# A two-layer decoder trunk on one core: where x is kept, how one of Strassen's sums is made, what is loaded first, two parts of w_so and the last norm

## The chip, the core and the metric

The kernel is one program on one of the eight cores of a Trainium2 chip. The core has a matrix engine (PE, TensorE), a vector engine (DVE), a scalar engine (ACT), a general engine (POOL, GpSimd) and a sequencer that mostly issues loads and stores (SP). Each engine runs its own instructions in a fixed order and waits on semaphores of the others; DMA queues move data between the device memory and the core's memory (SBUF). PE adds up its results in eight banks (PSUM) that DVE and ACT read. The metric is the device time of one execution in microseconds; the time before is 1018.95 us, the median of three runs.

## The reference

512 tokens of 1024 features go through two layers, all in float32. A layer is a mixer and an MLP, each with a scaled residual and a norm:

```python
for l in range(2):
    if l == 0:
        y = mla(x, w_in, g_q, g_kv, w_uq, w_uk, w_uv, w_o)      # 8 heads, latent keys and values, causal
    else:
        k_band, v_band = shared_kv(x, w_kv)                     # once
        y = swa(x, w_q, sinks, w_so, k_band, v_band, rel_bias)  # 16 heads, window 128, sinks
    x = layernorm(sqrt(2) * x + y, ln_mix_g[l], ln_mix_b[l])
    h = relu(x @ w_up[l])                                       # 1024 -> 4096
    x = layernorm(sqrt(2) * x + (h * h) @ w_down[l], ln_mlp_g[l], ln_mlp_b[l])
```

## The kernel before

**Split products.** A float32 operand is written as a high and a low part (`split`, L76: ACT rounds the high part, L78, DVE or POOL subtracts it, L81). A product is then three matmuls, high by high, high by low, low by high (`three`, L101; `group`, L95, issues them, so nearly all matmuls have line L97). In the profile `xth`, `xtl` are the parts of the features, `wh`, `wl` those of a weight, `fac` both parts of the MLP's hidden features, `oh`, `ol` those of a head pair's output.

**The stream of weights.** All weights are queued in one list, `stream`, in the order in which PE uses them. A tile (128x1024) is loaded into `raw` by SP and split into a ring of four `wh`, `wl` pairs; `weights` (L276) hands out the next pair and prepares up to four ahead. A split into the ring must wait until PE has read the old content of its place for the last time. The MLP uses Strassen's seven products for quarters of the up and down matrices (`queue_seven`, L147): their sums of quarters grow in place in `wq` by DMAs that POOL issues and that add to what is there (L170), each followed by a split of the grown tile.

**Layer A's mixer.** The features of x arrive transposed (xT) and are loaded and split piece by piece together with w_kv, then w_q, each on SP's queue and in the order of the program. The compressed keys and queries are normed (L802 on), transposed and kept as `ckv_h`, `ckv_l`, `cq_h`, `cq_l`; `pair_rotary` (L946) turns the rotary part of a pair of heads from `qrot` through one of the two banks for transposes (`tr`). `run_steps` (L475) sets the order by hand: scores some units ahead, softmax, mix, and between them `fill` entries, which are other PE work. The output matrix w_o is in parts, `proj.part(t, kp)`, for token tile t and two of eight heads kp.

**Norms.** `layer_norm` (L362) takes mean and variance on DVE, adds epsilon on DVE (L369), takes the inverse root on POOL (L350), and scales on DVE (L380, L383). The last tile of the last norm is divided: 832 columns on DVE, 192 on ACT and POOL (L376 to L379), and out by SP and ACT. In layer A, x's token tiles are loaded after its mixer.

**The MLP.** Block q of four runs steps of up products (U'n) and down products (D'n) in the order of `STEPS`; the first block's are U'1 U'2 U'5 U'3 U'6 U'7 U'4 D'1 D'2. `XFactors` makes the seven sums of x's quarters: `XFactors.turn` (L584) transposes a token tile, and at the last tile L560 and L562 form part 3's sum, then parts 3, 6, 7, 4 are split one after the other. The results of U'6, U'7, U'4 become the quarters a11, a21, a22 of the hidden features, squared on ACT (L692 relu, L693 square), then split into `fac` (`factor`) for D'1. `up_out` (L666) takes the sums out of PSUM on DVE.

Banks, rings and tiles are given out by a scheduler that puts each engine's instructions into one order before the run.

Of the kernel before, what the change touches and what calls it, by code (L numbers as in the profile page):

```python
# [8 lines left out]
F32 = mybir.dt.float32  # L9
# [6 lines left out]
P = 128  # L16
# [20 lines left out]
LN_CUT_END = 832  # L37

# [12 lines left out]
def build(tc, nc, io, out):  # L51
    with ExitStack() as top:
# [3 lines left out]
        sp = top.enter_context(tc.tile_pool(name="sp", bufs=1))  # L56
        ps = top.enter_context(tc.tile_pool(name="ps", bufs=1, space=PSUM))
# [18 lines left out]
        def split(dst_h, dst_l, src, engine=None, keep=False):  # L76

            high = nc.scalar.activation(dst_h, src, AF.Copy)  # L78
            if keep:
                pe(high)  # L80
            low = (engine or nc.vector).tensor_sub(dst_l, src, f32(dst_h))  # L81
            if pinned[0] and engine is None:
                pe(low)

# [3 lines left out]
        pinned = [False]  # L88

# [16 lines left out]

        def tiles_of_weights(aside=None):
# [10 lines left out]
        def queue(name, ap, low=nc.vector):  # L118


            def make(pieces=1, between=None):
                cols = ap.shape[-1]
                raw = raw_tile()
                wh, wl = tiles_of_weights()
                for j in range(pieces):
# [3 lines left out]
                    pe(nc.sync.dma_start(raw[:, c], ap[:, c]))  # L129
                    split(wh[:, c], wl[:, c], raw[:, c], low)  # L130
                return wh, wl

            stream.append((name, make))
# [13 lines left out]
        def queue_seven(name, key, chunk):  # L147
# [5 lines left out]
            def half(a, jp):  # L153
                if a not in quads:
                    if (key, a) == ("U", "a"):
                        quads[a] = xp.tile([P, 4, 512], F32, tag="xt", bufs=8, name=nm("wq"))
                    elif (key, a) == ("U", "b"):
                        quads[a] = xtok.tile([P, 4, 512], F32, tag="gb", bufs=1, name=nm("wq"))
# [7 lines left out]
            def grown(a, jp, *more, aside=None):  # L166
                wh, wl = tiles_of_weights(aside)
                split(wh, wl, flat(half(a, jp)), keep=(a, bool(more)) == ("b", True) and key == "U")
# [46 lines left out]
        queue("w_qr", io["w_qr"][0])  # L215
        queue("w_qr", io["w_qr"][1][:, 0:512])
# [102 lines left out]
        def load_x(k, n):  # L319
            at = k // 4, slice(k % 4, k % 4 + n)  # L320
            src = xraw[at[0]][:, at[1], :]
            nc.sync.dma_start(src, io["xT"][:, k : k + n, :])
# [10 lines left out]
        nc.sync.dma_start(ident, io["ident"])  # L333
        gq = cp.tile([P, 3], F32, name="gq")
        nc.sync.dma_start(gq, io["g_q"])
        gkv = cp.tile([P, 2], F32, name="gkv")
        nc.sync.dma_start(gkv, io["g_kv"])
        sink = cp.tile([P, SQH], F32, name="sink")
        nc.sync.dma_start(sink, io["sinks"].partition_broadcast(P))
        relb = cp.tile([33, SQH], F32, name="relb")  # L340
        nc.gpsimd.memset(relb[32:33, :], 1.0)
        nc.sync.dma_start(relb[0:32, :], io["rel"])
# [13 lines left out]
        def load_gb(g, b):  # L356
            gb = xtok.tile([P, 2, D], F32, tag="gb", bufs=1, name=nm("gb"))
# [4 lines left out]
        def layer_norm(t, gb, dst):  # L362
# [8 lines left out]
            end = dst is None and t == NT - 1  # L371
            cut = LN_CUT_END if end else D
            a, b = slice(0, cut), slice(cut, D)
            if end:
                shift = sp.tile([P, 1], F32, tag="v", bufs=8, name=nm("v"))
                nc.vector.tensor_scalar(shift, mv[:, 0:1], r, -1.0, ALU.mult, ALU.mult)  # L376
                nc.scalar.activation(x[:, b], x[:, b], AF.Identity, bias=shift, scale=r)
                nc.gpsimd.tensor_mul(x[:, b], x[:, b], gb[:, 0, b])
                nc.gpsimd.tensor_add(x[:, b], x[:, b], gb[:, 1, b])  # L379
            pin(nc.vector.scalar_tensor_tensor(x[:, a], x[:, a], mv[:, 0:1], gb[:, 0, a], ALU.subtract, ALU.mult))  # L380
            pieces = [slice(0, cut // 2), slice(cut // 2, cut)] if end else [a]
            for c in pieces:
# [3 lines left out]
            if end:  # L386
                nc.scalar.dma_start(out[t * P : (t + 1) * P, b], x[:, b])
# [22 lines left out]
        class TokMajor:  # L410
# [25 lines left out]
            def finish(self, gb=None, dst=None, early=None):  # L436
# [7 lines left out]
                if gb is not None:  # L444
                    ws = [weights(self.name) for _ in range(4)]
                    for t in range(NT):
# [28 lines left out]
        def run_steps(units, ahead, scores, turn, mix, fill, per, lag):  # L475
# [17 lines left out]
            for f in fill[at:]:  # L493
                f[3]()
            for u in range(n, n + lag):
# [5 lines left out]
        def count(t, c):  # L501
# [4 lines left out]
            for i in range(c.start // n, c.stop // n):  # L506
                pin(nc.vector.bn_stats(stats[t][:, i, :], xs[t][:, i * n : (i + 1) * n]))  # L507

# [60 lines left out]
        class XFactors(Factors):  # L569
# [14 lines left out]
            def turn(self, t):  # L584
                half_, tk = t // 2, slice(t % 2 * P, (t % 2 + 1) * P)
                if t % 2 == 0:
# [11 lines left out]
                if half_ == 1:  # L598
# [3 lines left out]
                    split(self.part(5, 0)[:, :, tk], self.part(5, 1)[:, :, tk], self.a[:, :, tk], keep=True)  # L602
                if t == NT - 1:
                    state["hold"] = len(stream)
                    quarters = [f32(self.xf[i][:, n]) for i in range(2) for n in range(2)]
                    for n in (3, 6, 7, 4):
                        split(self.part(n, 0), self.part(n, 1), self.sum(n, *quarters))

        def mlp(src, gb, dst, mp):
# [17 lines left out]
            class Block:  # L627
# [38 lines left out]
                def up_out(self, n, i):  # L666
# [114 lines left out]
        with tc.tile_pool(name="mla", bufs=1) as mp:  # L781
            const = mp.tile([P, C_ALL], F32, name="const")
            nc.sync.dma_start(const, io["const"])
# [4 lines left out]
            ckv_l = mp.tile([P, 2, S], F32R, name="ckv_l")  # L788
            khh = mp.tile([P, S], F32R, name="khh")
            kll = mp.tile([P, S], F32R, name="kll")  # L790
            cq_h = mp.tile([P, 3, S], F32R, name="cq_h")
# [570 lines left out]
```

## Time and profile before

| | |
|---|---|
| median of the runs | 1018.95 us (1017.45 to 1023.35) |
| the profiled execution | 1022.03 us, span 1020.2 us |
| mean granted clock of PE | 0.995 |
| PE busy, idle in the span | 995.0 us, 25.2 us |
| DVE, ACT, POOL busy | 766.3, 555.2, 229.9 us |
| software queue, accumulating loads of up | 64 of 512 KB, median 8.6 us to landing |

A row of the timeline has start, length, engine, line, operation, output<-input, shapes and count, and in brackets the idle time of the engine before it with what ended it. A row of the windows gives, for a stretch of time, the busy microseconds (and count) of each engine, then PE's granted clock, the DMA engines' share and their GB/s.

### The profile page before, as it was taken

How to read it: one execution, taken by the hardware profiler on the slowest of the kernel's cores; microseconds unless marked ns; L12 is line 12 of the kernel's file. 1: busy time of each engine (PE TensorE's matmuls, PEld its weight loads, DVE VectorE, ACT ScalarE, POOL GpSimd, SP SyncE). 2: the span in 40 equal slices, each digit the busy share in tenths (PEclk: the TensorE clock that was granted, in tenths of full speed). 3: DMA queues.
4: the chain of work that ended last, by engine and by line, in shares of the span. 5: the costliest groups of instructions: out<-in, count | busy, mean ns of one | idle time of the engine just before them, and what ended most of it. 6: DMA issues, size and time to landing. Idle time of an engine off the chain costs nothing. (4 is left out here: it accounts for less than half of the span.)

```text
span 1020.2 us, 15872 instructions
## 1 busy us (share of the span) xinstructions
PE 995.0 (98%) x6148; PEld 894.7 (88%) x6148; DVE 766.3 (75%) x1230; ACT 555.2 (54%) x848; POOL 229.9 (23%) x204
## 2 busy tenths in 40 slices
PE   8999999999999999999999999999999999999996
PEld 7878887898989989998889888889999999998985
DVE  4688875979869858887595578588886885798746
ACT  4446653457637636646145689445764664564620
POOL 0121100321211211220013665223032132122002
PEclk9999999999999999999999999999999999999999
DMA  6531116397986986973332223237798798798422
GB/s 211 159 99 45 52 42 231 59 247 195 198 182 186 194 182 171 252 138 109 99 103 94 66 81 114 81 86 201 169 219 179 164 222 167 167 264 150 108 99 82
DMA packets 60391, 149.55 MB, mean 147 GB/s; under 512 B 5228, under 2 KB 10141, under 8 KB 60317
## 3 DMA queue, kind: packets, MB, share of 16 engines
q0 software_dynamic: 24320, 58.73, 32.3%
q1 hardware_dynamic: 35852, 89.72, 26.3%
q8 instruction: 48, 0.79, 0.3%
q14 instruction: 27, 0.21, 0.1%
q10 hardware_dynamic: 144, 0.10, 0.0%
HBM read 146.41 MB, written 4.22 MB: 148 GB/s over the span
## 5 line engine op out<-in xcount | busy, mean ns | idle before, releaser
L97 PE MATMUL mm<-wh,fac 128*128 128x512 f32 (+1 forms) x944 | 293.0, 387 | 0.4 <-DVE fac L81 0.4
L78 ACT ACTIVATE wh<-wq 128x1024 fp32r<-128x1024 f32 x164 | 173.1, 1059 | 191.9 <-PE mm L97 123.9
L81 DVE TENSOR_TENSOR wl<-wq,wh 128x1024 fp32r<-128x1024 f32 x164 | 199.4, 1221 | 76.7 <-ACT wh L78 75.8
L97 PE MATMUL mm<-xth,wh 128*128 128x256 f32 (+1 forms) x936 | 245.8, 290 | 0.6 <-DVE a L687 0.5
L97 PE MATMUL mm<-xth,wl 128*128 128x256 f32 (+1 forms) x808 | 235.4, 291 | 0.0
L97 PEld LDWEIGHTS mm<-wh,fac 128*128 128x128 f32 x944 | 176.1, 188 | 36.6 <-DVE fac L81 1.9
L97 PE MATMUL mm<-xtl,wh 128*128 128x256 f32 (+1 forms) x680 | 199.7, 294 | 3.5 <-DVE xtl L81 3.5
L97 PE MATMUL mm<-wl,fac 128*128 128x512 f32 (+1 forms) x472 | 182.3, 386 | 0.0
L97 PEld LDWEIGHTS mm<-xth,wh 128*128 128x128 f32 x936 | 170.8, 192 | 4.0 <-issue 0.9
L97 PEld LDWEIGHTS mm<-xth,wl 128*128 128x128 f32 x808 | 155.4, 192 | 2.3
L78 ACT ACTIVATE wh<-raw 128x1024 fp32r<-128x1024 f32 (+4 forms) x89 | 87.9, 989 | 105.1 <-PE mm L97 59.2
L170 POOL DMA_DIRECT2D wq<-in_up x64 | 77.5, 1225 | 266.4 <-DVE wl L81 197.8
L97 PEld LDWEIGHTS mm<-xtl,wh 128*128 128x128 f32 x680 | 130.9, 192 | 7.1 <-DVE xtl L81 4.1
L81 DVE TENSOR_TENSOR wl<-raw,wh 128x1024 fp32r<-128x1024 f32 (+4 forms) x70 | 80.2, 1154 | 52.1 <-ACT wh L78 52.0
L97 PEld LDWEIGHTS mm<-wl,fac 128*128 128x128 f32 x472 | 88.8, 188 | 16.7
L170 POOL DMA_DIRECT2D wq<-in_down x48 | 42.0, 874 | 190.5 <-DVE wl L81 170.3
L350 POOL TENSOR_TENSOR rs<-v,half 128x1 f32<-128x1 f32 x24 | 28.6, 1190 | 201.5 <-DVE v L369 160.7
L81 POOL TENSOR_TENSOR wl<-raw,wh 128x1024 fp32r<-128x1024 f32 (+1 forms) x19 | 40.1, 2117 | 85.2 <-ACT wh L78 85.2
L97 PE MATMUL mm<-wl,oh 128*128 128x512 f32 x128 | 50.1, 391 | 0.7 <-DVE wl L81 0.7
L97 PE MATMUL mm<-wh,oh 128*128 128x512 f32 x128 | 50.7, 396 | 0.0
L97 PE MATMUL mm<-wh,ol 128*128 128x512 f32 x128 | 50.1, 391 | 0.0
L513 DVE TENSOR_TENSOR x<-mm,x 128x512 f32<-128x512 f32 (+1 forms) x49 | 32.9, 675 | 13.9 <-PE mm L97 13.6
(220 smaller groups left out, 1838.9 us busy)
## 6 DMA issues: line engine op xcount, KB each, us to landing
wq<-in_up POOLq DMA_DIRECT2D x64, 512.0 KB, 8.6
wq<-in_down POOLq DMA_DIRECT2D x48, 512.0 KB, 7.0
wq<-in_up SPq DMA_DIRECT2D x32, 512.0 KB, 5.8
raw<-in_down SPq DMA_DIRECT2D x28, 512.0 KB, 7.3
wq<-in_down SPq DMA_DIRECT2D x24, 512.0 KB, 7.1
raw<-in_up SPq DMA_DIRECT2D x16, 512.0 KB, 4.9
raw<-in_w_o SPq DMA_DIRECT2D x8, 512.0 KB, 3.3
raw<-in_w_sq SPq DMA_DIRECT2D x8, 512.0 KB, 3.4
```

Of the source, the lines that this page charges most:

```text
L78: high = nc.scalar.activation(dst_h, src, AF.Copy)
L81: low = (engine or nc.vector).tensor_sub(dst_l, src, f32(dst_h))
L97: pe(nc.tensor.matmul(dst, st, mv, start=first and i == 0, stop=last and i == len(pairs) - 1, **kw))
L170: nc.gpsimd.dma_start(half(a, jp), chunk(*more, jp), accum_op=ALU.add)
L350: nc.gpsimd.tensor_tensor(r, v, half, ALU.pow)
L513: nc.vector.tensor_add(xs[t][:, c], b, xs[t][:, c])
```

## The change

x's token tiles get their own pool, whose four places hold layer A's queries (`cq`, `qrot`) until the last of them is read; so x is loaded before layer A's end, and the mixer's gamma and beta after four more weight tiles. At the start the loads of w_kv's last two and w_q's four tiles go ahead of the small constants, through two tiles of the ring `xt` that are unused so far (`fetch`), and `pe` fixes SP's order. w_qr's low parts are subtracted by POOL. `pair_rotary` uses a bank of the matmuls. Epsilon is added to one of the batch statistics, so that the inverse root follows the variance directly. The last norm runs on DVE, in one pass and then two halves. Part 3's sum is built from a difference made at the start of the last turn, in two halves; parts 6, 7 and 4 move into `rest`, called by the first block's U'5 and ordered behind the last weight split issued by then. Two parts of w_o run before the last mix, and two parts of w_so some heads earlier.

```diff
-        queue("w_qr", io["w_qr"][0])
-        queue("w_qr", io["w_qr"][1][:, 0:512])
+        queue("w_qr", io["w_qr"][0], nc.gpsimd)
+        queue("w_qr", io["w_qr"][1][:, 0:512], nc.gpsimd)
...
+        spare = [xp.tile([P, 2, 1024], F32, tag="xt", bufs=8, name=nm("spare")) for _ in range(2)]
         for kp in range(1, 4):
             load_x(2 * kp, 2)
+            if kp > 1:
+                fetchers[kp](spare[0][:, kp - 2, :])
             prep(kp)
+        for i in range(4, 8):
+            fetchers[i](spare[1][:, i - 4, :] if i < 6 else raw_tile())
...
-            v = sp.tile([P, 1], F32, tag="v", bufs=8, name=nm("v"))
-            pin(nc.vector.tensor_scalar(v, mv[:, 1:2], LN_EPS, None, ALU.add))
-            r = rsqrt_of(v)
...
+            r = rsqrt_of(mv[:, 1:2])
+            pin(nc.vector.scalar_tensor_tensor(x, x, mv[:, 0:1], gb[:, 0, :], ALU.subtract, ALU.mult))
+            n = 2 if dst is None and t == NT - 1 else 1
+            for i in range(n):
+                c = slice(i * D // n, (i + 1) * D // n)
                 pin(nc.vector.scalar_tensor_tensor(x[:, c], x[:, c], r, gb[:, 1, c], ALU.mult, ALU.add))
...
+                if t == NT - 1:
+                    self.b = self.scratch()
+                    with tc.issue_after(self.low[1].ins):
+                        nc.vector.tensor_sub(self.b, f32(self.xf[0][:, 1]), f32(self.xf[0][:, 0]))
...
                 if t == NT - 1:
+                    for i in (1, 0):
+                        tk = slice(i * P, (i + 1) * P)
+                        if i == 0:
+                            with tc.issue_after(self.low[1].ins):
+                                nc.vector.tensor_add(self.b[:, :, tk], self.b[:, :, tk], self.a[:, :, tk])
+                        state["s4"] = split(self.part(3, 0)[:, :, tk], self.part(3, 1)[:, :, tk], self.b[:, :, tk], keep=True)
                     state["hold"] = len(stream)
-                    quarters = [f32(self.xf[i][:, n]) for i in range(2) for n in range(2)]
-                    for n in (3, 6, 7, 4):
-                        split(self.part(n, 0), self.part(n, 1), self.sum(n, *quarters))
+
+            def rest(self):
+
+                a11, _, a21, a22 = [f32(self.xf[i][:, n]) for i in range(2) for n in range(2)]
+                with behind(state["last"]):
+                    nc.vector.tensor_sub(self.a, self.a, a11)
+                    split(self.part(6, 0), self.part(6, 1), self.a)
+                    nc.vector.tensor_sub(self.b, a11, a21)
+                    split(self.part(7, 0), self.part(7, 1), self.b)
+                    split(self.part(4, 0), self.part(4, 1), a22)
...
                     w = [weights("up") for _ in range(2)]
+                    if (self.q, n) == (0, 5):
+                        src.rest()
...
                         if i == 1:
-                            nc.scalar.activation(self.g["a12"], self.g["a12"], AF.Square)
+                            with behind(state.pop("s4") if self.q == 0 else None):
+                                nc.scalar.activation(self.g["a12"], self.g["a12"], AF.Square)
...
+            cq = [xtok.tile([P, 2, S], F32R, tag="x", bufs=NT, name=nm("cq")) for _ in range(2)]
+            cq.append(mp.tile([P, 2, S], F32R, name="cq2"))
+            qrot = [xtok.tile([P, 2, 512], F32, tag="x", bufs=NT, name=nm("qrot")) for _ in range(2)]
+
+            def load_x_tokens():
+                for t in range(NT):
+                    xs[t] = xtok.tile([P, D], F32, tag="x", bufs=NT, name=nm("x"))
+                    pe(nc.sync.dma_start(xs[t], io["x"][t * P : (t + 1) * P, :]))
...
-                pt = tbank()
+                pt = bank()
...
+            fill.append((0, 99, -9, load_x_tokens))
...
+            run_steps([(h, i) for h in range(H) for i in range(NT)], AHEAD_S, scores, turn, mix, fill, NT, 2,
+                      [lambda kp=kp: proj.part(2, kp) for kp in range(2)])
...
-                    fill.append((1.3, 99, (11, 14)[t] + kp, lambda t=t, kp=kp: proj.part(t, kp)))
+                    at = 11 if (t, kp) < (0, 2) else (11, 14)[t] + kp
+                    fill.append((1.3, 11 if at == 11 else 99, at, lambda t=t, kp=kp: proj.part(t, kp)))
```

Three places show what this does to the order on an engine. The first is ACT in layer A's MLP, around the sums of x's quarters. `uv_456_2232` is part 3's sum before, `uv_449_2158` part 6's, `xf_446_2145` part 7's source; the `wq` tiles are the grown sums of w_up. Before:

```order
L78 ACTIVATE wh_461_2274<-wq_460_2272 128x1024
L78 ACTIVATE wh_463_2280<-wq_460_2272 128x1024
L78 ACTIVATE xth_457_2236<-uv_449_2158 128x1024
L78 ACTIVATE xth_450_2160<-uv_456_2232 128x1024
L78 ACTIVATE wh_465_2285<-wq_407_1908 128x1024
L78 ACTIVATE xth_459_2243<-xf_446_2145 128x1024
L78 ACTIVATE wh_469_2340<-wq_407_1908 128x1024
L78 ACTIVATE wh_471_2345<-wq_460_2272 128x1024
```

and of the change, where part 3's sum is `uv_452_2215` and part 6's `uv_447_2157`:

```order
L77 ACTIVATE xth_448_2159<-uv_452_2215 128x4x128 x2
L724 ACTIVATE a12_451_2213<-a12_451_2213 128x1024
L77 ACTIVATE wh_456_2266<-wq_455_2264 128x1024
L77 ACTIVATE wh_458_2272<-wq_455_2264 128x1024
L77 ACTIVATE wh_460_2277<-wq_408_1912 128x1024
L77 ACTIVATE wh_467_2343<-wq_408_1912 128x1024
L77 ACTIVATE xth_462_2283<-uv_447_2157 128x1024
L77 ACTIVATE wh_469_2348<-wq_455_2264 128x1024
```

Part 3 stands ahead of the weights now, in two halves; part 6 stands behind `wh_460_2277` and `wh_467_2343`, the two weight tiles of U'6. On DVE, too, `wl_468_2344` comes just ahead of part 6's low half.

The second place is ACT at the change from U'4 to D'1. `fac_491_2533` before and `fac_489_2536` after are the first hidden factor (a11's) that D'1 multiplies; the `raw` tiles hold D'1's second pair of weights. Before:

```order
L693 ACTIVATE a11_481_2435<-a11_481_2435 128x1024
L692 ACTIVATE a21_489_2503<-a21_489_2503 128x1024
L78 ACTIVATE fac_491_2533<-a11_481_2435 128x1024
L78 ACTIVATE fac_498_2601<-a12_453_2214 128x1024
L78 ACTIVATE wh_495_2544<-raw_494_2542 128x1024
L693 ACTIVATE a21_489_2503<-a21_489_2503 128x1024
L78 ACTIVATE wh_500_2606<-raw_499_2604 128x1024
```

and of the change:

```order
L739 ACTIVATE a21_487_2506<-a21_487_2506 128x1024
L77 ACTIVATE wh_493_2547<-raw_492_2545 128x1024
L740 ACTIVATE a11_479_2438<-a11_479_2438 128x1024
L740 ACTIVATE a21_487_2506<-a21_487_2506 128x1024
L77 ACTIVATE wh_498_2609<-raw_497_2607 128x1024
L77 ACTIVATE fac_489_2536<-a11_479_2438 128x1024
L77 ACTIVATE fac_496_2604<-a12_451_2213 128x1024
```

Both weight splits stand ahead of the factor now. The place in the ring that `wh_498_2609` takes was held by U'4's second weight tile. Layer B's MLP has the same two orders.

The third is SP at the start, before:

```order
L322 DMA xraw_7_90<-in_xT 128x1024 x2
L333 DMA ident_133<-in_ident 128x128
L335 DMA gq_135<-in_g_q 128x3
L337 DMA gkv_137<-in_g_kv 128x2
L129 DMA raw_14_118<-in_w_kv 128x640
L339 DMA sink_139<-in_sinks 128x16
L342 DMA relb_141<-in_rel 32x16
L783 DMA const_153<-in_const 128x1024
L856 DMA qrot_161<-in_oh 33x384
L129 DMA raw_17_127<-in_w_kv 128x640
L129 DMA raw_26_192<-in_w_q 128x768
```

and of the change:

```order
L343 DMA xraw_7_93<-in_xT 128x1024
L148 DMA spare_11_109<-in_w_kv 128x640
L343 DMA xraw_7_93<-in_xT 128x1024
L148 DMA spare_11_109<-in_w_kv 128x640
L148 DMA spare_12_110<-in_w_q 128x768 x2
L148 DMA raw_20_138<-in_w_q 128x768
L148 DMA raw_21_140<-in_w_q 128x768
L359 DMA ident_142<-in_ident 128x128
L361 DMA gq_144<-in_g_q 128x3
```

The six weight loads no longer stand behind a place in `raw` that must come free, nor behind the constants.

More of the change, by code (lines that the diff above doesn't have):

```diff
@@ L83, in split @@
                 pe(low)
+            return high, low
         def pe(ins):
@@ L88, in build, with behind @@
         pinned = [False]
+        def behind(pair):
+            both = ExitStack()
+            for ins in pair or ():
+                both.enter_context(tc.issue_after(ins.ins))
+            return both
         def pin(ins):
@@ L167, in grown @@
                 wh, wl = tiles_of_weights(aside)
-                split(wh, wl, flat(half(a, jp)), keep=(a, bool(more)) == ("b", True) and key == "U")
+                with behind(state.get("s4") if (key, a, jp, bool(more)) == ("U", "b", 0, True) else None):
+                    state["last"] = split(
+                        wh, wl, flat(half(a, jp)), keep=(a, bool(more)) == ("b", True) and key == "U"
+                    )
                 if more:
@@ L494, in run_steps @@
                 f[3]()
+            for f in rest:
+                f()
             for u in range(n, n + lag):
@@ L1243, in build @@
             values(0)
-            run_steps([(h, 0) for h in range(SQH)], AHEAD_B, scores, turn, mix, fill, 1, 1)
-        gb = load_gb(io["ln_mix_g"][1], io["ln_mix_b"][1])
+            run_steps([(h, 0) for h in range(SQH)], AHEAD_B, scores, turn, mix, fill, 1, 1, [])
+        gb = lambda: load_gb(io["ln_mix_g"][1], io["ln_mix_b"][1])
         with tc.tile_pool(name="mlp1", bufs=1) as mp:
```

97 lines of the change are left out of this document (47 added, 50 removed).

## The prediction

> **What bounds the kernel.** First the page's head, then PE's waits by releaser.
>
> ```profile
> span 1020.2 us, 15872 instructions
> PE 995.0 (98%) x6148; PEld 894.7 (88%) x6148; DVE 766.3 (75%) x1230; ACT 555.2 (54%) x848; POOL 229.9 (23%) x204
> ```
>
> ```profile
> PE mm L97 <- DVE xtl L81: 3.5, 3, 1.3
> PE tr L1192 <- DVE ptl L81: 2.7, 3, 2.3
> PE mm L97 <- DVE v L804: 1.7, 2, 1.1
> ```
>
> PE sets the time almost throughout: 25.2 us of 1020.2 are idle, so removing a wait on PE gains its length and a new one costs it. The change leaves PE's matmuls the same in number, so I read only waits. One more thing costs PE time without being idle, its clock. The windows:
>
> ```profile
> 21.70:26.40 4.70, 3.04 (x15) 2.14 (x13) 2.69 (x9) 2.30 (x6) 0.56 (x1) 1.00 0.33 115
> 26.40:29.80 3.40, 3.34 (x10) 3.34 (x11) 3.26 (x15) 1.68 (x5) 1.10 (x2) 0.50 0.50 155
> ...
> 214.13:217.54 3.41, 2.07 (x18) 1.87 (x17) 2.65 (x3) 1.83 (x3) 2.21 (x2) 1.00 1.08 296
> 217.54:220.95 3.41, 3.41 (x31) 3.41 (x30) 3.31 (x3) 1.21 (x3) 1.19 (x1) 1.00 1.13 218
> 531.56:534.98 3.42, 1.88 (x12) 1.26 (x12) 3.29 (x7) 2.78 (x7) 0.00 (x0) 1.00 0.46 153
> 534.98:538.39 3.41, 3.41 (x18) 3.41 (x18) 2.14 (x5) 0.58 (x2) 0.00 (x0) 0.50 0.00 0
> ```
>
> Where PE idled 1.66 us (4.70 less 3.04) or 1.54 us in a stretch, the next 3.4 us were granted 0.50; after 1.34 us idle they stayed at 1.00. A stall of over about 1.5 us thus costs, by these rows, half of 3.4 us again: 1.7.
>
> **Start: -3.3.** The wait on L804 stands for w_q's splits, whose loads SP reaches late:
>
> ```profile
> 3.54 0.91 SPq L322 DMA_DIRECT2D xraw<-in_xT  x2
> ...
> 14.74 9.54 SPq L129 DMA_DIRECT2D raw<-in_w_q  x4
> ```
>
> SP is held there by places in `raw`, which come free with the splits. The change issues all four behind the xT pieces, which end at 4.45: at 0.46 us an issue the six loads are out by about 8. That frees the 1.66 us and the half-speed window behind it (1.7): -3.3. Bounds: 0, if the six loads only crowd xT, and -3.3.
>
> **Layer A's attention: -2.6.** Four gaps:
>
> ```profile
> 53.00 0.66 PE L814 MATMUL tr<-ident,p 128*128 128x128 f32 x4 [1.21 <-DVE cq_l L816]
> ...
> 79.50 0.41 PE L1020 MATMUL tr<-ident,p 128*128 128x128 f32 x2 [1.03 <-DVE qr L954]
> ...
> 156.26 0.50 PE L97 MATMUL mm<-pt,vh 128*128 128x512 f32 x1 [0.69 <-ACT pt L78]
> 156.99 0.50 PE L97 MATMUL mm<-pt,vh 128*128 128x512 f32 x1 [0.22 <-DVE pt L81]
> ```
>
> At 53.00 DVE had just made two splits of w_qr, which go to POOL:
>
> ```profile
> 49.26 1.23 DVE L81 TENSOR_TENSOR wl<-raw,wh 128x1024 fp32r<-128x1024 f32 x1 [1.10 <-ACT wh L78]
> 51.00 0.68 DVE L81 TENSOR_TENSOR wl<-raw,wh 128x512 fp32r<-128x512 f32 x1
> ```
>
> Only the second lies directly ahead: -0.7 (bounds -1.2 and 0). The transposes at 79.50 waited for a bank; with one of the other six, -1.0. Before the last mix 12 matmuls of w_o cover 0.9. x's loads and the norms' chain, one small DVE step shorter, lie beside busy PE: 0; uncovered, the one would cost a load's few us, since w_o's tiles queue behind it on SP.
>
> **The MLP's U'3: -2.7.** PE waited 1.34 us for part 3 in each layer:
>
> ```profile
> 216.84 0.39 PE L97 MATMUL mm<-xtl,wh 128*128 128x256 f32 x1 [1.34 <-DVE xtl L81]
> ...
> 707.89 0.39 PE L97 MATMUL mm<-xtl,wh 128*128 128x256 f32 x1 [1.34 <-DVE xtl L81]
> ```
>
> ```profile
> 208.74 0.69 DVE L81 TENSOR_TENSOR xtl<-uv,xth 128x512 fp32r<-128x512 f32 x1 [0.70 <-ACT xth L78]
> 209.46 1.23 DVE L560 TENSOR_TENSOR uv<-uv,xf 128x1024 f32<-128x1024 f32 x1
> 210.72 1.23 DVE L562 TENSOR_TENSOR uv<-xf,uv 128x1024 f32<-128x1024 f32 x1
> ...
> 214.43 2.35 DVE L81 TENSOR_TENSOR xtl<-uv,xth 128x1024 fp32r<-128x1024 f32 x2
> ```
>
> Now one half addition and two half splits (0.69 each, as the first row) follow 209.43: ready by about 212, needed at 215.5. Both gaps go.
>
> **U'6: +2.9 and +1.7.** Here is what is late next. Part 6 now stands behind U'6's own second weight tile on ACT and DVE. That tile was
>
> ```profile
> 216.55 1.06 ACT L78 ACTIVATE wh<-wq 128x1024 fp32r<-128x1024 f32 x1 [1.58 <-DMA wq<-in_up]
> ...
> 220.75 1.06 ACT L78 ACTIVATE wh<-wq 128x1024 fp32r<-128x1024 f32 x1 [2.20 <-DMA wq<-in_up]
> ```
>
> released at 220.75 by the load that POOL issued from 206.1 on, the second of
>
> ```profile
> 204.94 2.44 POOL L170 DMA_DIRECT2D wq<-in_up  x2 [3.07 <-DVE wl L81]
> ```
>
> U'6 began at
>
> ```profile
> 222.57 0.28 PE L97 MATMUL tr<-xth,wh 128*128 128x256 f32 x1
> ```
>
> and is now wanted 1.34 earlier, at 221.23. ACT starts part 6 at 221.7 (conversions follow each other by 0.95) and ends at 222.75; DVE makes the weight's low half 221.84 to 223.0, then part 6's, to 224.2. The first matmul is 1.5 late, the second waits again, together 2.9. In layer B the same tile is released at 710.53 and U'6, as far behind U'3 as in layer A (5.73), is wanted at 707.89 + 5.73 - 1.34 = 712.28: 714.0 for the low half, +1.7.
>
> ```profile
> 710.53 1.06 ACT L78 ACTIVATE wh<-wq 128x1024 fp32r<-128x1024 f32 x1 [1.67 <-DMA wq<-in_up]
> ```
>
> The bounds are 0 (the load lands 3 us earlier) and these sums; that load took 14.6 us against a median of 8.6 on the page:
>
> ```profile
> wq<-in_up POOLq DMA_DIRECT2D x64, 512.0 KB, 8.6
> ```
>
> I take the sums, as the change issues it in the same crowd: the DMA share was 1.08 and 1.13 in the windows above. The Trainium skill, "DMA: Bandwidth & Descriptors", section "Anatomy of one DMA — SWDGE (gpsimd) path", fits 2.0 us plus bytes over 436 GB/s for one load, 3.2 us for 512 KB as an estimate; by it the wait would not exist, but the trace's 8.6 and 14.6 disagree.
>
> **D'1: +2.85 in each layer.** D'1's first product needs a11's factor. Before, ACT made both factors ahead of the `raw` tiles:
>
> ```profile
> 238.91 1.99 ACT L78 ACTIVATE fac<-a 128x1024 fp32r<-128x1024 f32 x2
> 240.80 1.04 ACT L78 ACTIVATE wh<-raw 128x1024 fp32r<-128x1024 f32 x1
> ```
>
> ```profile
> 240.42 0.40 PE L97 MATMUL mm<-wh,fac 128*128 128x512 f32 x1
> ...
> 241.26 0.73 PE L97 MATMUL mm<-wh,fac 128*128 128x512 f32 x2 [0.21 <-DVE fac L81]
> ```
>
> Now the second `raw` split stands ahead of the factor, and its ring place is read by U'4's last matmul, the one ahead of 240.42, done at about 240.6. So: split 240.6, factor's high half 241.55 to 242.6, D'1 begins 2.2 us late. On DVE the weight's low half runs 241.7 to 242.9, the factor's 242.85 to 244.1, where the third matmul, before at 241.26, waits: +2.85. Queued behind that split on ACT are both factors and a22's squares. Bounds +0.9 (the place is free earlier, ACT is only two conversions later: the first rival) and +3.8 (another conversion falls in between).
>
> **Clock: +5.9.** Both D'1 stalls (3.2 us idle in 3.5) and U'6 in layer A (2.9) must fill a window: 3 x 1.7; U'6 in layer B, 1.7 us that a boundary may divide, half of it, 0.8.
>
> **Layer B's w_so: +0.5.** The two parts cover the 2.3 us wait on L1192. But the part that follows now comes straight behind a mix, and needs POOL's `ol`:
>
> ```profile
> 637.61 1.28 POOL L81 TENSOR_TENSOR ol<-o,oh 128x512 fp32r<-128x512 f32 x1 [2.51 <-ACT oh L78]
> 638.85 0.40 POOL L1179 TENSOR_TENSOR p<-p,ri 128x128 f32<-128x128 f32 x1
> 639.21 1.47 POOL L1181 TENSOR_TENSOR p<-p,ri 128x768 f32<-128x768 f32 x1
> ```
>
> The chain of mix, ACT, DVE, ACT, POOL is as long as before, and PE is 2.7 us of matmuls shorter ahead of it: the gap moves. If the two `p` steps come first, 1.87 more. Bounds -2.5 (the cover works and nothing waits behind it) and +1.9; I take +0.5, near the moved gap, since `ol` ended at 638.89 when its matmul was due just then.
>
> **Tail: -1.3.** The last store left at
>
> ```profile
> 1014.43 1.21 DVE L383 SCALAR_TENSOR_TENSOR x<-x,rs,gb 128x416 f32<-128x416 f32 x2
> ...
> 1016.77 0.38 ACTq L387 DMA_DIRECT2D out<-x  x1
> ```
>
> Two halves of 512 on DVE (1.21 x 512/416 = 1.49) from about 1014.2, since a small step ahead of them goes: the store leaves at about 1015.6, 1.2 earlier; with the norm's other small step I take 1.3. Bounds -1.5 and 0.
>
> **The sum.** -3.3 - 2.6 - 2.7 - 1.3 = -9.9; +4.6 + 5.7 + 5.9 + 0.5 = +16.7; together +6.8: the profiled execution's 1022.03 becomes 1028.8, its span 1027.0. The runs' median lies 3.1 below the profiled execution, so the forecast is 1018.95 + 6.8 = 1025.8, in its own range 1021 to 1031.
>
> **Rivals.**
> *The two conversions do not wait (0.23).* U'6 and D'1 lose by one thing: on ACT a weight split that may wait stands ahead of an operand. If it is ready when ACT gets there (the load lands by 218, as 8.6 us from 206.1 would have it, and the ring place is free before U'4 ends), the only cost is order: D'1 0.9 each, no window. Then -9.9 + 1.8 + 0.5 = -7.6: 1011.4. For it: the median landing, and conversions' usual 0.95 spacing. Against: the ring has four places, and the order gives this one to U'4's second tile.
> *The stalls come, the clock stays (0.09).* +6.8 - 5.9 = +0.9: 1019.8. The Trainium skill, "TensorE: Matmul & The Clock Gate", section "Part 1: The HAM clock gate (the "warmup" mystery)", has the clock halved after a whole idle window of about 3.4 us; none of these stalls fills one, and by that rule this rival would hold. Against it stand the rows with 1.66 and 1.54 idle.
> *More is late (0.18).* The six first loads take DMA time from xT, so that the start gains nothing (+3.3), and each D'1 stall touches two windows (2 x 1.7): +13.5, 1032.4. For it: both stalls of D'1 spread over 3.5 us. Against: SP still issues xT's pieces first.
> *S4 is not earlier after all:* if the early difference waits for a `uv` place, U'3's 2.7 us stay, within the ranges.
>
> **Chances.** The measurement cannot tell less than about 0.5% (5.1 us) from no change: faster is below 1013.9, slower above 1024.0. The forecast has 0.50, of which 0.10 falls below 1024.0. Faster 0.23; within 0.10 + 0.09 = 0.19; slower 0.40 + 0.18 = 0.58. Both signs hold chance, so the range goes from below the first rival to above the third: 1010 to 1033.
>
> **What would show it.** In the changed profile: no half clock at 26 us and w_q's four loads on SP before 10; no idle time before U'3; two waits on `xtl` at the start of U'6, behind a conversion released by a DMA; at D'1 about 2.2 us on ACT's `fac` and 1 on DVE's, with 0.50 granted in the window behind. If D'1 begins within 1 us of U'4's end, the forecast is wrong and the first rival right; if it stalls at 1.00, the second.

## The result, and the profile after

| | before | after |
|---|---|---|
| median of 20 runs each, side by side | 1018.93 us (1017.15 to 1023.35) | 1026.56 us (1021.62 to 1036.02) |
| ratio of the times | | 1.0069, 95% interval 1.0052 to 1.0087 |
| profiled execution, its span | 1022.03, 1020.2 us | 1029.26, 1027.2 us |
| mean granted clock of PE | 0.995 | 0.990 |

The kernel became slower by 0.7%: 7.6 us between the medians, 7.0 between the spans; the forecast was 1025.8, +6.8. First the changed kernel's head and its list of PE's waits by releaser (us in total, times, the longest):

```profile
span 1027.2 us, 15878 instructions
PE 1000.3 (97%) x6148; PEld 897.7 (87%) x6148; DVE 768.4 (75%) x1233; ACT 556.4 (54%) x849; POOL 219.1 (21%) x204
```

```profile
PE mm L104 <- ACT fac L77: 4.4, 2, 2.4
PE tr L104 <- DVE xtl L80: 2.1, 2, 1.1
PE mm L104 <- DVE wl L80: 1.8, 3, 0.9
PE mm L104 <- POOL ol L80: 1.8, 1, 1.8
PE mm L104 <- DVE fac L80: 1.4, 2, 0.7
```

PE's idle time is 26.9 us (1027.2 less 1000.3), before it was 25.2: nearly as much as ever. The same 6148 matmuls took 5.3 us more. 4.7 of it is half clock: the halved windows that only one of the two traces has hold 12.7 us of busy PE after and 3.4 before, and half of the difference is lost. The other 0.6 is a sum of small differences of both signs and was not taken apart. So waits were exchanged for other waits, and the new ones brought stretches at half clock. Both of U'3's waits (1.34) are gone; U'6 now waits on part 6, D'1 on its factor. (The page of waits lists one 1.2 on `xtl` in a `mm` row too; that one stands at the start of layer B, not at U'3.)

The ledger below sets the two traces side by side at the same matmul. It gives when the changed kernel reached it, less when the old one did, and so how much each place added:

| from, to (us in the trace before) | difference at its end | added | predicted |
|---|---|---|---|
| start, to 34 | -3.1 | -3.1 | -3.3 |
| layer A's attention, to 162 | -6.6 | -3.5 | -2.6 |
| w_o's last tile, 177 | -5.5 | +1.1 | 0 |
| U'3 of layer A, 217 | -7.0 | -1.5 | -1.35 |
| U'6: waits, then half clock | -4.7, -3.1 | +2.3, +1.6 | +2.9, +1.7 |
| U'4, where the kernel before waits 0.35 | -3.6 | -0.6 | 0 |
| D'1: waits, then half clock | -0.9, none | +2.7, 0 | +2.85, +1.7 |
| D'1's later wait and layer B's first stage, 535 | +0.7 | +1.6 | 0 |
| w_so, with its half clock, 668 | +2.4 | +1.6 | +0.5 |
| U'3 of layer B, 708 | +0.9 | -1.5 | -1.35 |
| U'6 of layer B, 714, half clock | +2.2, none | +1.3, 0 | +1.7, +0.8 |
| D'1 of layer B: waits, then half clock, to the last matmul | +5.5, +8.4 | +3.3, +2.9 | +2.85, +1.7 |
| tail | +7.0 | -1.4 | -1.3 |

The timeline of PE shows the new waits as rows (start, length, engine, line, what; in brackets the idle time ahead and what ended it):

```profile
171.20 0.50 PE L104 MATMUL mm<-wl,oh 128*128 128x512 f32 x1 [0.94 <-DVE wl L80]
...
216.57 0.38 PE L104 MATMUL tr<-xth,wh 128*128 128x256 f32 x1 [0.84 <-ACT xth L77]
...
218.02 0.51 PE L104 MATMUL tr<-xtl,wh 128*128 128x256 f32 x1 [1.07 <-DVE xtl L80]
...
238.93 0.50 PE L104 MATMUL mm<-wh,fac 128*128 128x512 f32 x1 [1.99 <-ACT fac L77]
...
240.38 0.74 PE L104 MATMUL mm<-wh,fac 128*128 128x512 f32 x2 [0.72 <-DVE fac L80]
```

What stood ahead of them is in ACT's timeline. First around U'6, where part 6's conversion (`xth<-uv`) starts 0.96 behind a weight's that a DMA released; then around D'1:

```profile
214.51 1.06 ACT L77 ACTIVATE wh<-wq 128x1024 fp32r<-128x1024 f32 x1 [2.60 <-DMA wq<-in_up]
215.47 1.04 ACT L77 ACTIVATE xth<-uv 128x1024 fp32r<-128x1024 f32 x1
```

```profile
231.10 1.06 ACT L77 ACTIVATE wh<-wq 128x1024 fp32r<-128x1024 f32 x1 [1.82 <-PE mm L104]
232.07 1.99 ACT L739 ACTIVATE a<-a 128x1024 f32<-128x1024 f32 x2
234.03 1.06 ACT L77 ACTIVATE wh<-raw 128x1024 fp32r<-128x1024 f32 x1
235.00 1.99 ACT L740 ACTIVATE a<-a 128x1024 f32<-128x1024 f32 x2
236.89 1.04 ACT L77 ACTIVATE wh<-raw 128x1024 fp32r<-128x1024 f32 x1
237.84 1.99 ACT L77 ACTIVATE fac<-a 128x1024 fp32r<-128x1024 f32 x2
```

From 231.10 on ACT has no idle time. From the first `relu` (L739) to the factor it makes six operations, 0.95 apart, where the trace before shows four:

```profile
235.09 1.06 ACT L692 ACTIVATE a<-a 128x1024 f32<-128x1024 f32 x1 [2.14 <-DVE a L684]
236.06 1.04 ACT L78 ACTIVATE wh<-wq 128x1024 fp32r<-128x1024 f32 x1
237.01 1.04 ACT L693 ACTIVATE a<-a 128x1024 f32<-128x1024 f32 x1
237.96 1.04 ACT L692 ACTIVATE a<-a 128x1024 f32<-128x1024 f32 x1
```

The two more are the `raw` split at 236.89 and a second square. The words "D'1's second pair" in the part on the change are not right for these `raw` tiles: they are D'2's, prepared ahead. The order shown there is right, and the wait comes where it was said to.

The windows of the changed kernel (stretch, length, busy us and count of PE, PEld, DVE, ACT, POOL, then the granted clock) show where the half clock followed:

```profile
214.71:218.13 3.42, 1.51 (x11) 1.11 (x10) 3.10 (x3) 2.81 (x4) 1.00 (x1) 1.00 1.13 207
218.13:221.54 3.41, 3.41 (x17) 3.41 (x18) 3.33 (x3) 2.89 (x4) 0.20 (x1) 0.50 1.13 206
235.19:238.61 3.42, 1.75 (x15) 1.55 (x13) 2.50 (x3) 3.42 (x4) 0.00 (x0) 1.00 1.05 211
238.61:242.02 3.41, 2.37 (x9) 1.67 (x10) 2.97 (x4) 3.23 (x4) 0.00 (x0) 1.00 0.77 210
...
637.97:641.38 3.41, 1.64 (x7) 0.72 (x6) 2.21 (x7) 3.36 (x13) 2.89 (x3) 1.00 0.01 2
641.38:644.79 3.41, 3.19 (x8) 2.41 (x9) 0.34 (x2) 0.29 (x3) 1.99 (x3) 0.50 0.00 0
733.54:736.95 3.41, 0.95 (x4) 0.32 (x3) 2.49 (x4) 3.41 (x4) 0.00 (x0) 1.00 1.03 199
736.95:740.36 3.41, 2.71 (x6) 2.15 (x7) 2.98 (x3) 2.15 (x3) 0.00 (x0) 0.50 0.71 229
740.36:743.78 3.42, 3.42 (x9) 2.64 (x8) 2.30 (x4) 1.06 (x1) 0.00 (x0) 0.50 0.95 343
```

The first window had 1.91 us of idle PE (3.42 less 1.51) and the next was halved. Layer A's D'1 stall, 2.71 us in all, fell on a window's boundary: 1.67 and 1.04 idle, no drop. The stall at the same place in layer B, 3.16 us, fell mostly into one window, 2.46, and two halved windows followed.

### The profile page after: what moved, and what is told of

Its sections match the earlier page's. It is cut to its first block, busy times and chain, and to the rows that moved or that the text cites. A ratio compares the mean times of both kernels' runs of the same rounds, so it can differ in the third digit from the quotient of the medians.

```text
span 1027.2 us, 15878 instructions
## 1 busy us (share of the span) xinstructions
PE 1000.3 (97%) x6148; PEld 897.7 (87%) x6148; DVE 768.4 (75%) x1233; ACT 556.4 (54%) x849; POOL 219.1 (21%) x204
## 4 chain that ended last, share of the span: by engine, by line
PE 85%; DMA 5%; DVE 4%; ACT 3%; issue 1%; SPq 0%; POOL 0%; DVEq 0%; ACTq 0%; POOLq 0%
PE mm L104 78%; PE tr L104 4%; DMA wq<-in_up 3%; DVE wl L80 1%; ACT wh L77 1%; DMA xraw<-in_xT 1%; DMA gb<-in_ln_mix_b 1%; PE tr L1075 1%; DMA raw<-in_w_o 1%; PE tr L1245 1%; DMA raw<-in_w_v 1%; PE tr L623 1%; ACT a L740 0%; PE tr L1247 0%; DVE x L400 0%
## 5 line engine op out<-in xcount | busy, mean ns | idle before, releaser
L77 ACT ACTIVATE wh<-raw 128x1024 fp32r<-128x1024 f32 (+4 forms) x85 | 84.8, 998 | 92.7 <-PE mm L104 57.6
L80 DVE TENSOR_TENSOR wl<-raw,wh 128x1024 fp32r<-128x1024 f32 (+3 forms) x64 | 74.9, 1177 | 48.0 <-ACT wh L77 47.8
L80 POOL TENSOR_TENSOR wl<-raw,wh 128x1024 fp32r<-128x1024 f32 (+2 forms) x21 | 43.8, 2090 | 81.2 <-ACT wh L77 81.1
L377 POOL TENSOR_TENSOR rs<-mv,half 128x1 f32<-128x1 f32 x16 | 11.1, 691 | 169.4 <-DVE mv L393 169.4
```

Source lines behind the costliest of these rows:

```text
L377: nc.gpsimd.tensor_tensor(r, v, half, ALU.pow)
```

## The experiments

All times are medians beside runs of the kernel before on the same chip. The first four edit the changed kernel, each at one place.

**One split behind D'1's factor.** Only the order of ACT and DVE at D'1 changes.

```diff
-                    split(f[:, 0], f[:, 1], g[2] if n == 0 else self.down.sum(n, *g))
+                    pair = split(f[:, 0], f[:, 1], g[2] if n == 0 else self.down.sum(n, *g))
+                    if (self.q, n) == (0, 1):
+                        state["fac1"] = pair
...
-                    w = [weights("down") for _ in range(2)]
+                    with behind(state.pop("fac1") if (self.q, n) == (0, 1) else None):
+                        w = [weights("down") for _ in range(2)]
```

> Theory (order on ACT): the 2.0 and 2.4 us that PE waits for ACT's factor at D'1 come only from the weight split that stands ahead of it. With that one split behind the factor, D'1 begins about 0.9 us late at most and its second wait of 0.7 goes: 2 x 1.8 us less idle, and the half-speed windows behind layer B's D'1 (two in the changed kernel's profile) go: 3.4 us more. About 1019.5 us against 1026.6. Rival A (the factor is late by itself): D'1 still waits over 1.5 us, 1026. Rival B (the half speed does not hang on these stalls): only the idle time goes, 1023, and the profile still shows half speed at 737 us. Rival C (the split is now itself late): D'2 waits for its second weight tile, 1024.

Measured: 1024.17 us, ratio 1.0046 (1.0029 to 1.0063). PE's timeline in layer A:

```profile
237.64 0.50 PE L104 MATMUL mm<-wh,fac 128*128 128x512 f32 x1 [1.04 <-ACT fac L77]
238.90 0.50 PE L104 MATMUL mm<-wh,fac 128*128 128x512 f32 x1 [0.53 <-DVE fac L80]
```

The wait on ACT fell from 1.99 to 1.04, in layer B from 2.44 to 1.48: by 0.95 and 0.96, one conversion's spacing, and no more. The split does not wait for its ring place; it takes its turn. By the rows above, the rest of the stall is the longer chain ahead of it (the second square, and a start 0.5 us later against U'4's end); no run took these two apart. The expected 1019.5 was missed for that, and because the shorter stall, 1.57 us, now fell into one window and was followed by half clock in layer A too (239.6 to 243.0 at 0.50).

**Part 6 freed.** Part 6's difference and split come out of the order behind U'6's weight tiles; parts 7 and 4 stay.

```diff
+                nc.vector.tensor_sub(self.a, self.a, a11)
+                split(self.part(6, 0), self.part(6, 1), self.a)
                 with behind(state["last"]):
-                    nc.vector.tensor_sub(self.a, self.a, a11)
-                    split(self.part(6, 0), self.part(6, 1), self.a)
```

> Part 6's sum and split are no longer held behind U'6's second weight tile (parts 7 and 4 still are). Theory: U'6's two waits (1.9 us in layer A, 1.1 in layer B) and the half-speed window behind the first go, about 4.5 us; and since the order of D'1 on ACT also returns to factor first, the gain of the run that moves only that comes on top: about 1015 us. Rival A (part 6 taken early delays part 3 or a weight split on ACT, so that U'3 or U'6 waits for that instead): 1019 to 1020, no better than with D'1's order alone. Rival B (the load, not the order, sets U'6): U'6 still waits 1 us or more for its own weight tile.

Measured: 1020.82 us, ratio 1.0009 (0.9991 to 1.0027), a miss against the expected 1015. Both waits at U'6 are gone, so their cause was the weight ahead of part 6. But PE's list has a new first row, U'4, and D'1 still waits:

```profile
PE mm L104 <- DVE a L734: 4.5, 2, 2.3
PE mm L104 <- ACT fac L77: 3.0, 2, 1.5
```

L734 is DVE's sum that reads U'7's result from the bank into which U'4 then adds. DVE's timeline ahead of it:

```profile
224.04 1.23 DVE L80 TENSOR_TENSOR wl<-wq,wh 128x1024 fp32r<-128x1024 f32 x1 [1.00 <-ACT wh L77]
225.18 0.68 DVE L729 TENSOR_TENSOR uv<-mm,uv 128x512 f32<-128x512 f32 x1
225.78 0.68 DVE L728 TENSOR_TENSOR uv<-tr,uv 128x512 f32<-128x512 f32 x1
226.56 1.23 DVE L80 TENSOR_TENSOR wl<-wq,wh 128x1024 fp32r<-128x1024 f32 x1
227.70 0.68 DVE L731 TENSOR_TENSOR a<-mm,uv 128x512 f32<-128x512 f32 x1
228.30 0.68 DVE L729 TENSOR_TENSOR uv<-mm,uv 128x512 f32<-128x512 f32 x1
228.90 0.68 DVE L734 TENSOR_TENSOR a<-uv,mm 128x512 f32<-128x512 f32 x1
```

The sums are behind the low parts of later weights, of which the first was itself held 1.00 us. The wait went from part 6 to the next thing in line.

**The clock, with the stall left.** Eight products of zeros go into D'1's bank ahead of its first product. They add nothing to the result and fill the idle time.

```diff
+                        if (self.q, n, t) == (0, 1, 0):
+                            group(b, [(zeros[:, :P], zeros[:, P:])] * 8)
```

> Eight matmuls of zeros (1.8 us of PE) are put into the bank of D'1's first product ahead of it, in both layers; they are overwritten by it. PE has to wait there anyway. Theory (clock by idle time in a window of 3.4 us): the waits for the factor shrink from 2.0 and 2.4 us to about 0.2 and 0.6, the time of the stall stays, and the two half-speed windows behind layer B's D'1 go: 3 us less, 1023.5 us. Rival (half speed has another cause, or the fillers take time themselves): the same or up to 3.6 us more, 1026.5 to 1030, with 0.50 granted behind 737 us as before.

Measured: 1023.89 us, ratio 1.0051 (1.0036 to 1.0066), granted clock of the profiled execution 0.995. PE's timeline in layer A, and the window with layer B's D'1 and the next:

```profile
234.76 1.99 PE L104 MATMUL mm<-zeros 128*128 128x512 f32 x8
...
237.01 0.50 PE L104 MATMUL mm<-wh,fac 128*128 128x512 f32 x1 [0.25 <-ACT fac L77]
```

```profile
731.97:735.38 3.41, 2.08 (x9) 1.11 (x8) 2.67 (x4) 3.41 (x4) 0.00 (x0) 1.00 0.95 219
735.38:738.80 3.42, 3.42 (x16) 2.81 (x17) 2.77 (x3) 2.10 (x3) 0.00 (x0) 1.00 0.77 283
```

The factor comes as late as before; only PE is busy while it waits. Layer B's window has 1.33 us of idle PE in place of 2.46, and the next stayed at 1.00; no half clock stood at either D'1. By the ratios 0.2% is gone, about 1.8 us, where the ledger puts layer B's two windows at 2.9. The two ratios' intervals overlap, so the time alone would not carry this; the windows do. The mean clock of this one execution would not either: U'6's stall in layer A brought no half clock here, as a window's boundary divided it.

**The two parts of w_so put back.**

```diff
-                    at = 11 if (t, kp) < (0, 2) else (11, 14)[t] + kp
-                    fill.append((1.3, 11 if at == 11 else 99, at, lambda t=t, kp=kp: proj.part(t, kp)))
+                    fill.append((1.3, 99, (11, 14)[t] + kp, lambda t=t, kp=kp: proj.part(t, kp)))
```

> The two parts of w_so go back to their old place, the rest of the change stays. Theory: ahead of the transposes PE waits 2.3 us again, as before the change, but the 1.8 us for ol, the 0.9 us of small waits around it and the half-speed window at 641 us go: 0 to 2 us less, 1025 us. Rival (moving the parts gains): 1028 to 1029, with 2.3 us of wait more and no wait less.

Measured: 1025.37 us, ratio 1.0066 (1.0051 to 1.0081). By the time it cannot be told from the changed kernel. The 2.3 us wait on `ptl` is back and the 1.80 on `ol` is gone: one for the other, as the prediction had it. The half clock moved with them, from 641 us to the window behind the `ptl` wait (626.67 to 630.08 at 0.50). POOL's timeline in the changed kernel shows that the worse of its two orders came about, the long `p` step ahead of `ol`:

```profile
638.85 1.47 POOL L1234 TENSOR_TENSOR p<-p,ri 128x768 f32<-128x768 f32 x1
640.28 1.27 POOL L80 TENSOR_TENSOR ol<-o,oh 128x512 fp32r<-128x512 f32 x1
```

**The other parts alone.** Four kernels in one series. The kernel before with the early first loads alone (the edits of `queue`, `fetch` and SP's order as in the diff of the change):

> The kernel before with the early loads of w_kv and w_q alone. Theory: the wait at 24 to 26 us and the half-speed window behind it go, 3.3 us; the changed kernel shows PE 3.1 to 3.6 us ahead of the one before from 33 us on: 1015.6 us. Rival (the gain is lost later, since what follows waits for other loads): under 1 us of it is left at 60 us.

Measured: 1017.08 us, ratio 0.9972 (0.9962 to 0.9982): by the ratio -2.9, against a forecast of -3.3.

The changed kernel with part 3's sum, `turn` and the order around them as before:

```diff
...
-                if t == NT - 1:
-                    self.b = self.scratch()
...
-                        nc.vector.tensor_sub(self.b, f32(self.xf[0][:, 1]), f32(self.xf[0][:, 0]))
...
+                    quarters = [f32(self.xf[i][:, n]) for i in range(2) for n in range(2)]
+                    for n in (3, 6, 7, 4):
+                        split(self.part(n, 0), self.part(n, 1), self.sum(n, *quarters))
...
-                        src.rest()
...
```

> The changed kernel with part 3's sum, and the places of parts 6, 7 and 4, as before the change. Theory (the losses in the MLP come from the order that this piece brings): U'3 waits 1.3 us in each layer again, and the waits at U'6 (1.9 and 1.1), at D'1 (2.7, 0.6 and 3.2) and their half-speed windows (three in the profile) go: 2.7 back, 9.5 + 5.1 gone, 1014.5 us. Rival (those waits are the price of being early elsewhere, they come whatever the order): 1024 us or more, with waits of 2 us at U'4 or D'1 as in the run that freed part 6.

Measured: 1015.42 us, ratio 0.9960 (0.9945 to 0.9976). The waits at U'6 and D'1 are gone (the longest left there is below 0.25), and U'3's are back:

```profile
211.57 0.38 PE L104 MATMUL mm<-xtl,wh 128*128 128x256 f32 x1 [1.34 <-DVE xtl L80]
```

So this one part of the change accounts for 11 us: 1026.56 against 1015.42 (two series; each has its own runs of the kernel before, by the ratios it is 1.1%). It saves 2.7 and costs what U'6, D'1 and the clock add.

The same with w_so's two parts put back as well:

> As the run before in this list, and w_so's two parts at their old place. Theory: 1 to 2 us less than that, 1013 us, as the two pieces act at different places. Rival (w_so's parts gain once the rest is in order): 1 to 2 us more.

Measured: 1013.02 us, ratio 0.9930 (0.9907 to 0.9953). That is near the expected 1013, but the interval overlaps that of the run before, so what w_so's parts cost there is not shown.

And with the split of w_o's last tile on ACT and DVE put ahead of that of the first grown tile, which removes the 1.30 us wait that this kernel had where the changed one had 0.94:

```diff
-                    split(wh[:, c], wl[:, c], raw[:, c], low)
+                    state["lastq"] = split(wh[:, c], wl[:, c], raw[:, c], low)
...
-                with behind(state.get("s4") if (key, a, jp, bool(more)) == ("U", "b", 0, True) else None):
+                with behind(state["lastq"] if aside and (a, jp, bool(more)) == ("a", 0, True) else None):
```

> As the run before in this list, and on ACT and DVE the split of w_o's last tile stands ahead of the split of the first grown tile of the MLP, which waits for a load. Theory (the 0.9 us wait at 171 us is again a conversion that waits ahead of one that is wanted): it goes, 0.9 us in layer A and up to 0.75 in layer B: 1011.5 to 1012 us. Rival (w_o's last tile itself lands late): the wait stays, 1013 us.

Measured: 1012.67 us, ratio 0.9926 (0.9908 to 0.9943), the lowest median of all, 7.5 us ahead of the kernel before by the ratio. Its profile has no half clock before PE's last matmul:

```profile
span 1009.5 us, 15867 instructions
PE 989.4 (98%) x6148; PEld 892.3 (88%) x6148; DVE 765.1 (76%) x1227; ACT 556.3 (55%) x847; POOL 216.8 (21%) x204
```

That execution is a good one. By the medians the reordering itself gave 0.35 us, which these runs cannot tell from nothing; that the wait at 171 is gone is what the trace shows. Its two longest waits both stand at w_so: 2.28 on `ptl`, as the old place of the parts has it, and 2.11 on `ol`, with POOL's two `p` steps just ahead of `ol` again. So the wait on `ol` hangs on POOL's order, and not on the place of the parts alone.

**The early sum, in other orders.** Two attempts to keep U'3's gain. The first takes that last kernel with the early sum and puts parts 6, 7 and 4 straight behind part 3:

```diff
+                    self.rest()
...
-                with behind(state["last"]):
+                with behind(state["s4"]):
...
-                        src.rest()
```

> As the last run of the list before (w_so's parts at the old place, w_o's last split first), with part 3's sum made early as in the change, but parts 6, 7 and 4 split straight behind it and not in the first block's U'5. Theory (the early sum gains, only the place of the rest loses): U'3's 1.3 us go in both layers, 1010 us. Rival A (the two sums of 1.2 us now delay U'3's weights on DVE): U'3 waits about as long as before, for a low half of its weight: 1012.5. Rival B (the loads limit what follows): what U'3 gains is waited for at U'4, 1012.5, with 1.5 us or more there.

Measured: 1023.22 us, ratio 1.0042 (1.0023 to 1.0062): a clear miss, 13 us above the expectation. U'3 and U'6 do not wait, but U'4 does, 3.33 us in layer A and 2.21 in layer B, half clock behind both; that is the wait of rival B, longer than it put. D'1 waits 1.2 in each layer. First PE's row, then DVE's timeline and ACT's:

```profile
228.81 0.47 PE L104 MATMUL mm<-xth,wh 128*128 128x256 f32 x2 [3.33 <-DVE a L735]
```

```profile
223.31 1.23 DVE L80 TENSOR_TENSOR wl<-wq,wh 128x1024 fp32r<-128x1024 f32 x1 [2.46 <-ACT wh L77]
224.45 0.69 DVE L730 TENSOR_TENSOR uv<-mm,uv 128x512 f32<-128x512 f32 x1
```

```profile
222.22 1.06 ACT L77 ACTIVATE wh<-wq 128x1024 fp32r<-128x1024 f32 x1 [3.22 <-DMA wq<-in_up]
```

A weight's load landed at 222.2. ACT waited 3.22 us for it, DVE 2.46 us for ACT, and a sum that reads a bank (L730) stood behind. Its last input had been ready since the sum at 220.17, so it lost over 3 us to its place in the order.

The second, otherwise as that last kernel, puts `rest` between U'5's two weight tiles, and the splits made in U'7's step (of U'4's second tile and D'1's first) behind the last sum of U'6:

```diff
-                    w = [weights("up") for _ in range(2)]
-                    if (self.q, n) == (0, 5):
-                        src.rest()
+                    with behind(state.pop("u6") if (self.q, n) == (0, 7) else None):
+                        w = [weights("up")]
+                        if (self.q, n) == (0, 5):
+                            src.rest()
+                        w.append(weights("up"))
```

> As s4_early, but parts 6, 7 and 4 stand behind U'3's second weight tile (in the change: behind U'6's first, and so behind its second), and the splits of U'4's second tile and D'1's first stand behind the sums that U'6 leaves on DVE. Theory (all the MLP's losses are order): U'3 and U'6 do not wait, U'4 waits under 0.7 us, D'1 under 1 us: 1009.5 us. Rival (the loads limit it): 1.5 to 2 us of wait at U'4 for its own first weight tile in both layers, 1012 to 1013.

Measured: 1014.97 us, ratio 0.9947 (0.9929 to 0.9966); the expected 1009.5 was missed. U'3 and U'6 do not wait, U'4 waits 0.77 and 0.36 in layer A, D'1 1.45 in each layer on DVE's factor. It beats the changed kernel by 1.2%. Of the same kernel without the early sum (ratio 0.9926) it is 0.2% short, and the intervals overlap: no gain of the early sum is shown.

## Why the prediction was right

**What bounds.** PE's idle and busy time make up the whole difference, with the matmuls equal in number: idle +1.7, busy +5.3, of which 4.7 is half clock, together the span's +7.0. The places of the large terms and their signs were right. That the sum is within 0.2 is luck: the ledger's rows miss their forecasts by about 5.7 us upward and as much downward.

**U'6, right and 0.6 to 1.0 too large in layer A.** The mechanism is as written: a weight tile released by a DMA stands ahead of part 6 on ACT, two waits, the first on ACT, the second on DVE. The load landed 1.2 us ahead of the time PE wanted U'6 (214.51 against 216.57 - 0.84 = 215.73), where 0.5 was forecast; that makes 1.9 of waiting instead of 2.9. Layer B measured 1.07 against 1.7. The freed part 6 removed these waits, so the cause is shown.

**D'1, right in size, half right in cause.** 2.71 and 3.16 us of waiting against 2.85. The step that failed is "the second `raw` split stands ahead of the factor, and its ring place is read by U'4's last matmul", as the whole cause. The split does stand there, and it was made just as U'4 ended, but ACT had no idle time ahead of it, so it waited for nothing, and undoing it returned only 0.95. By the rows, one more square and a later start made up the rest. The forecast met the number by luck, because U'4's end and ACT's free time fell together (236.94 and 236.99).

**Clock, right in sum, wrong in places.** Forecast were one window each for U'6 in layer A and both D'1, and half a window for U'6 in layer B, +5.9. There came one for U'6, none for layer A's D'1, two for layer B's, none for its U'6, and one at w_so that was not forecast at all: 1.6 + 2.9 and, as half of the 3.19 us busy in its window, 1.6, together +6.1. Errors of both signs cancelled. Where "a boundary may divide" was said of U'6 in layer B, it divided D'1 in layer A. The Trainium skill, "TensorE: Matmul & The Clock Gate", section "Part 1: The HAM clock gate (the "warmup" mystery)", would have the clock stay after stalls that fill no window; the halved windows behind 1.91 and 1.77 us of idle time disagree, and with them falls the rival "the stalls come, the clock stays".

**w_so.** The 2.28 wait was covered and the moved one came with POOL's steps in the worse order, 1.80 on `ol` beside three small waits (0.43, 0.29, 0.19). But three small waits of the kernel before (0.75, 0.27, 0.18) are gone there too: PE's idle time in that stretch, 620 to 669 us before, fell from 3.5 to 2.9, where +0.5 was forecast. What was missed is that the new wait, at 1.77 idle in one window, halves the next, 1.6 us.

**Start, U'3, tail: right**, within 0.2 us each: -3.1 for -3.3, -1.5 for -1.35 in each layer, -1.4 for -1.3. The start's gain is net of 1.0 that the first matmuls lost at 12 us. The pieces of xT took a median of 6.3 us to landing there, 4.4 before: a part of the bound "0, if the six loads only crowd xT". The last of w_q's four loads left SP at 12.2, not by about 8.

**Layer A's attention, 0.9 better than said; w_o's last tile, 1.1 worse.** The two nearly cancel. The second was costed at nothing: w_o's last split stood behind a grown tile's on ACT and DVE, and PE, arriving 6.6 us sooner, met it. Reordering it removed the wait. Of the +1.6 from D'1 to layer B's first stage, 0.9 comes with D'1's later wait on a sum (0.56, gone in the first experiment); 0.7 stands in waits at layer B's start that no run here took apart.

**The first rival** (the two conversions do not wait, 1011.4) fell at U'6, where the conversion waited for its load. At D'1 it was nearer the truth than the forecast: the conversion did not wait there. Only its price, 0.9, was too small, since two more operations stood ahead of the factor and their chain began later. The kernels without the early sum came near its time.

## What to carry to other kernels

On an engine with a fixed order, look at what an operand stands behind, not only at when its inputs are ready: a weight split that waits for a load or a ring place holds up every sum, bank and factor behind it. Moving a producer ahead only helps if the next two or three consumers are ready as well; here 2.7 us gained at U'3 came back as waits at U'6, U'4 or D'1 in each of the orders tried. Measure the parts of a change one at a time: the same change without the early sum of part 3 and the two parts of w_so was 0.7% faster than before, with them 0.7% slower.

## What the runs showed of the hardware

The granted clock changes in windows of 3.41 us with a fixed phase in each execution: in all twelve profiles its changes lie whole multiples of that apart. At full clock, a window of 1.77 us or more of idle PE was followed by one at 0.50 in every profile of this study, one of up to 1.50 in none; between them it went both ways (1.57 yes, the 1.67 above no; where matmuls end is modelled, so the exact bound stays open). Rows of the kernel without the early sum show one that just stays:

```profile
168.71:172.12 3.41, 1.91 (x9) 1.29 (x8) 3.41 (x9) 0.32 (x1) 1.35 (x1) 1.00 0.91 292
172.12:175.54 3.42, 3.42 (x17) 2.82 (x16) 2.58 (x5) 1.80 (x2) 0.56 (x1) 1.00 1.06 243
```

The same stall therefore costs nothing more or one window or two by where the boundary falls. While PE had work, two windows were halved in a row only where the first of them, already at 0.50, held idle time again: 0.70 us at layer B's D'1, and 0.66 at the same place in the kernel with w_so's parts put back. Every other halved window there had at most 0.44 and was followed by 1.00. Why a halved window needs less idle time to stay down is open. The phase is the likely reason that the changed kernel's 20 runs spread over 14.4 us, with mean clocks from 0.994 to 0.981 (0.013 of 1027 us is 13.4 us), against 6.2 us before. It has more stalls near the bound; that the phase changes from run to run is inferred from the clocks, not traced.
